# RWKV shift and gated-DeltaNet convolution read from PSUM, state copies by ScalarE, five kinds of stores on GpSimd's queue

## The chip, the cores and the metric

The kernel runs on one core of a Trainium2 chip. The metric is the time on the device of one execution, in microseconds (us). A core has five engines, each of which works through its own list of instructions in order: TensorE (PE, the matrix engine, whose results land in banks of PSUM), VectorE (DVE), ScalarE (ACT), GpSimd (POOL) and SyncE (SP, which here only issues transfers). They meet through semaphores: an instruction that waits holds up everything behind it on its engine.

## The reference

One step of a hybrid decoder of two layers, width 1024, on 512 prompt tokens and 32 sample tokens (8 sequences of 4) that share the weights. In each layer one projection `h @ w_in` is split into four mixers. Two parts of it matter here. RWKV mixes each token's projection with that of the token before it, and the gated DeltaNet runs a convolution of width 4 along time:

```python
prev = jnp.concatenate([shift_buf, p[:, :-1]], axis=1)      # rwkv7_mixer
xs = p + (prev - p) * prm['rw_mu']
...
xp = jnp.concatenate([buf, x], axis=1)                      # causal_dwconv
y = sum(xp[:, i:i + L] * w[i] for i in range(width))
return y, xp[:, L:]
```

The last row of `p` and the last three rows of `x` are outputs too (the new shift and convolution states). The sample tokens take their earlier rows from `state_rwkv_shift` and `state_gdn_conv`; the prompt starts from zeros.

## The kernel before

Everything is kept transposed: features on the 128 partitions, tokens along the free dimension. The tokens are worked on in two halves: half 0 is the prompt's first 256 columns, half 1 the other 256 and the 32 sample columns (288). So there are four projections, written (layer, half): (0,0), (0,1), (1,0), (1,1). In the execution shown, RWKV's and the DeltaNet's units are evacuated at about 24 to 78 us for (0,0), 141 to 213 us for (0,1), 640 to 697 us for (1,0) and 1037 to 1085 us for (1,1).

A projection is a row of units of 128 output features. A unit's weights come as two half units of 128x512 numbers (`load_part`): SP's queue loads one into `wraw` (five buffers), ScalarE rounds it into `whi`, VectorE subtracts to get `wlo` (three buffers each). TensorE makes 24 matmuls per unit in `dense`: high weights on the high and the low part of the input, low weights on the high part. They add up in one PSUM bank of the tag `mm`, of which there are three, so a unit's bank must be free again before the third unit after it can start. `evac` then takes the unit out of the bank.

`rw_evac` (units 0 to 7) and `gd_evac` (units 10 to 15) first copy the bank by ScalarE into a tile `raw` (shown as `e`) with room ahead of the columns for the row or rows before. GpSimd fills that room (zeros, or `rwlast` and `rwshift`, `gdlast` and `gdconv`) and copies the new states out at the end (`rwlast`, `rwshs`, `gdlast`, `gdcs`). ScalarE writes the scaled projection to `xs` or `cv`, and VectorE adds the shifted rows with one `scalar_tensor_tensor` per tap (`stt`, listed at line 245, the helper's), over `raw` whole.

A small ninth piece, `narrow`, loads 8 gate columns (`wnar`) through SP's queue, L1689. Also on SP's queue are the stores of two S5 tables (`m1` at L1337, `s5en` at L1396, both made by GpSimd in `tables`) and of the residual `x` at L1653.

The order on each engine is laid out by a scheduler when the program is built, from priorities that the sections carry (the evacuation's is 1050, the load's 294); the engines keep to it when they run.

Of the kernel before, what the change touches and what calls it, by code (L numbers as in the profile page):

```python
# [11 lines left out]
AF = mybir.ActivationFunctionType  # L12
ALU = mybir.AluOpType
# [3 lines left out]
DEPTH, D, SEQ, DB, DS = 2, 1024, 512, 8, 4  # L17
NS = DB * DS
# [121 lines left out]
class K:  # L140
# [16 lines left out]
    def t(self, shape, tag, bufs=1, dt=F32, pool="sb"):  # L157
# [1 line left out]
        return self.pool(pool).tile(list(shape), dt, tag=tag, name=f"{tag}_{self.n}", bufs=bufs)  # L159


    CLS = {"c0": (640, 7), "c1": (1152, 4), "e1": (1280, 2), "d1": (1152, 2), "d2": (2304, 2), "sums": (1152, 3),
           "xs": (9216, 1), "r2": (2304, 5), "r4": (4096, 5),
           "cv": (6912, 1), "gz": (2304, 1), "g2": (2304, 5), "g4": (4608, 1),
           "t2": (2048, 5), "s0": (4096, 1),
# [205 lines left out]
    def rw_evac(self, r, u, ps):  # L371

        nc = self.nc
        half, xs = r["half"], r["xs"]
        mu = self.p("rw_mu")[:, u:u + 1]
        om = self.rwd[:, u:u + 1]
        raw = self.w([128, 1 + 256 + DB + NS], "e1")
        self.acopy(raw[:, 1:257], ps[:, :256])
        if not half:
            nc.gpsimd.memset(raw[:, 0:1], 0.0)  # L380
        else:
            nc.gpsimd.tensor_copy(raw[:, 0:1], self.rwlast[:, u:u + 1])
            nc.gpsimd.tensor_copy(raw[:, 257:257 + DB], self.rwshift[:, u])
            self.acopy(raw[:, 257 + DB:], ps[:, 256:])
            self.act(xs[:, u, 256:], ps[:, 256:], AF.Copy, scale=om)
            self.stt(xs[:, u, 256:], raw[:, 257:257 + NS], mu, xs[:, u, 256:], ALU.mult, ALU.add)
            nc.gpsimd.tensor_copy(self.rwshs[:, u], raw[:, 257 + NS:])
        if u in (4, 5):

            sw = lambda a: a.rearrange("p (b c t) -> p b c t", b=2, c=2)  # L390
            xo, pi, pp = sw(xs[:, u, 0:256]), sw(raw[:, 0:256]), sw(ps[:, :256])
            for c in range(2):
                self.act(xo[:, :, 1 - c], pp[:, :, c], AF.Copy, scale=om)
                self.stt(xo[:, :, 1 - c], pi[:, :, c], mu, xo[:, :, 1 - c], ALU.mult, ALU.add)
# [372 lines left out]
    def gd_evac(self, r, u, ps):  # L767
        nc = self.nc
        half, cv = r["half"], r["cv"]
        w = lambda i: self.p("gdn_conv_w")[:, i * 6 + u:i * 6 + u + 1]  # L770
        raw = self.w([128, 3 + 256 + 3 * DB + NS], "e1")
        if not half:
            nc.gpsimd.memset(raw[:, 0:3], 0.0)  # L773
        else:
            nc.gpsimd.tensor_copy(raw[:, 0:3], self.gdlast[:, u])
            nc.gpsimd.tensor_copy(raw[:, 259:259 + 3 * DB], self.gdconv[:, u])
            self.acopy(raw[:, 259 + 3 * DB:], ps[:, 256:])
        self.acopy(raw[:, 3:259], ps[:, :256])
# [481 lines left out]
    def s5_tables(self, l):  # L1260
        nc = self.nc
        V = self.t([128, 16, 8], "s5v", bufs=1)
        k = lambda j: V[:, j]
# [13 lines left out]
        c1 = 6.28125  # L1277
# [42 lines left out]
        kx, m1 = (self.w([128, 2, 8, 16, 4], "r4") for _ in range(2))  # L1320
# [53 lines left out]
        en = self.w([128, 2, 8, 64], "r4")  # L1374
        nc.gpsimd.memset(en[:, 0, :, 0:1], 1.0)
        nc.gpsimd.memset(en[:, 1, :, 0:1], 0.0)
        w, cur, nxt = 1, (V[:, 14], V[:, 15]), (V[:, 12], V[:, 13])
        while w < 64:
# [3 lines left out]
            a = (en[:, 0, :, 0:w], en[:, 1, :, 0:w])  # L1382
            o = (en[:, 0, :, w:2 * w], en[:, 1, :, w:2 * w])
# [243 lines left out]
    def residual(self, half, src, sums, cls, final=False, wide=True):  # L1627


        c0, n = HALVES[half]  # L1630
        xt = self.fetch(half, cls)
        rs = self.rms(sums)
        step = 2 if final else 4
        new = None if final else self.row(half, "sums")
        mp = None
        for q in range(0, 8, step):
            a, xq = src[:, q:q + step], xt[q // 4][:, q % 4:q % 4 + step]
            self.tt(a, a, rs.unsqueeze(1).to_broadcast([128, step, n]))
# [401 lines left out]
```

## Time and profile before

| | |
|---|---|
| median of 3 runs | 1650.72 us (1645.68 to 1654.04) |
| profiled execution | 1647.81 us, span of the trace 1646.0 us |
| TensorE busy | 1560.8 us, 95% of the span |
| VectorE, ScalarE, GpSimd busy | 74%, 59%, 19% |
| mean granted TensorE clock | 0.978 |

The page's chain that ended last is of little use for this change, since it shows only the end. What tells is, stage by stage, how much of a window TensorE was idle, and what it waited for there.

### The profile page before, as it was taken

The numbers are of one execution on the slowest core, as the hardware profiler recorded it, in microseconds if no ns is written. First come the engines' busy times: TensorE is split into PE (matmuls) and PEld (weight loads), VectorE is DVE, ScalarE is ACT, GpSimd is POOL, SyncE is SP. The second block draws the span as 40 slices with busy tenths as digits, with TensorE's granted clock in tenths as the row PEclk, the third lists the DMA queues.
The fourth block names the chain that finished last, engine by engine and source line by source line (L and its number), as shares of the span: only waits on it lengthen the run. The fifth ranks groups of instructions, "written<-read, shape, count | busy, mean of one in ns | idle before, by whom it ended". The sixth has DMA issues, their size and how long they took to land. (4 is left out here: it accounts for less than half of the span.)

```text
span 1646.0 us, 38658 instructions
## 1 busy us (share of the span) xinstructions
PE 1560.8 (95%) x14464; PEld 1454.1 (88%) x14464; DVE 1210.5 (74%) x2865; ACT 964.8 (59%) x2094; POOL 311.5 (19%) x614
## 2 busy tenths in 40 slices
PE   6989999899999999799999999999999999999996
PEld 6878987788898999788889999989889989999996
DVE  6799775876786868778586667889768865866665
ACT  6676556653355468575455567876444456855544
POOL 4661232000230424600020002520002101100001
PEclk9999998899999999899999999999999999999998
DMA  6635443443466566435356546534534755665453
GB/s 216 198 108 130 150 152 122 119 107 111 140 217 213 194 206 232 129 94 148 117 179 194 164 161 208 176 125 139 151 113 148 250 194 194 205 193 167 160 170 103
DMA packets 205415, 267.36 MB, mean 162 GB/s; under 512 B 81114, under 2 KB 98844, under 8 KB 204812
## 3 DMA queue, kind: packets, MB, share of 16 engines
q1 hardware_dynamic: 203308, 258.73, 49.8%
q0 software_dynamic: 1920, 6.17, 1.0%
q8 instruction: 113, 1.85, 0.5%
q14 instruction: 74, 0.61, 0.1%
HBM read 237.95 MB, written 28.58 MB: 162 GB/s over the span
## 5 line engine op out<-in xcount | busy, mean ns | idle before, releaser
L232 ACT CAST whi<-wraw 128x512 fp32r<-128x512 f32 x752 | 463.0, 619 | 426.0 <-PE ps L220 267.4
L236 DVE TENSOR_TENSOR wlo<-wraw,whi 128x512 fp32r<-128x512 f32 x752 | 535.6, 718 | 211.6 <-ACT whi L232 189.3
L220 PE MATMUL ps<-h,whi 128*128 128x288 f32 (+1 forms) x3264 | 515.3, 297 | 9.3 <-ACT h L228 4.3
L220 PEld LDWEIGHTS ps<-h,whi 128*128 128x128 f32 x3264 | 451.7, 192 | 24.8 <-ACT h L228 5.7
L220 PE MATMUL ps<-f,whi 128*128 128x288 f32 (+1 forms) x2752 | 425.4, 294 | 6.9 <-ACT whi L232 2.8
L220 PEld LDWEIGHTS ps<-f,whi 128*128 128x128 f32 x2752 | 374.3, 190 | 19.8 <-issue 5.4
L220 PE MATMUL ps<-h,wlo 128*128 128x288 f32 (+1 forms) x1632 | 289.7, 296 | 3.0 <-DVE wlo L236 2.7
L220 PEld LDWEIGHTS ps<-h,wlo 128*128 128x128 f32 x1632 | 236.6, 191 | 12.8 <-DVE wlo L236 5.6
L220 PE MATMUL ps<-f,wlo 128*128 128x288 f32 (+1 forms) x1376 | 237.6, 294 | 6.4 <-DVE wlo L236 6.3
L220 PEld LDWEIGHTS ps<-f,wlo 128*128 128x128 f32 x1376 | 197.3, 190 | 11.6 <-DVE wlo L236 7.6
L236 POOL TENSOR_TENSOR sums<-sums,d 128x288 f32<-128x288 f32 (+1 forms) x60 | 60.9, 1016 | 530.7 <-ACT d L228 525.1
L236 DVE TENSOR_TENSOR acc<-acc,ps 128x256 f32<-128x256 f32 (+1 forms) x96 | 41.6, 434 | 52.9 <-PE ps L220 52.5
L220 PE MATMUL ps<-r,r 64*64 64x64 f32 (+7 forms) x1184 | 68.4, 237 | 10.3 <-DMA r<-s5m 3.3
L220 PEld LDWEIGHTS ps<-r,r 64*64 64x64 f32 (+4 forms) x1184 | 56.5, 141 | 20.3 <-issue 9.0
L232 ACT CAST f<-d 128x288 fp32r<-128x288 f32 (+1 forms) x128 | 53.4, 417 | 30.8 <-DVE d L236 30.4
L228 ACT ACTIVATE d<-ps 128x256 f32<-128x256 f32 (+1 forms) x156 | 61.3, 393 | 14.0 <-PE ps L220 12.8
L228 ACT ACT_TABLE_LOAD x45 | 57.7, 1283 | 0.8
L236 DVE TENSOR_TENSOR f<-d,f 128x288 fp32r<-128x288 f32 (+1 forms) x128 | 55.5, 433 | 2.9 <-ACT f L232 2.5
L236 DVE TENSOR_TENSOR d<-d 128x288 f32<-128x288 f32 (+1 forms) x128 | 55.7, 435 | 1.5 <-ACT d L228 1.5
L232 ACT COPY e<-ps 128x256 f32<-128x256 f32 (+2 forms) x96 | 27.9, 324 | 17.9 <-PE ps L220 8.4
L245 DVE SCALAR_TENSOR_TENSOR cv<-e,pf,cv 128x256 f32<-128x256 f32 (+1 forms) x90 | 32.4, 403 | 7.4 <-POOL e L773 4.3
L232 ACT COPY r<-ps 64x128 f32<-64x128 f32 (+2 forms) x56 | 20.4, 370 | 29.2 <-PE ps L625 12.1
(395 smaller groups left out, 1852.8 us busy)
## 6 DMA issues: line engine op xcount, KB each, us to landing
wraw<-in_w_up SPq DMA_DIRECT2D x256, 256.0 KB, 2.8
wraw<-in_w_down SPq DMA_DIRECT2D x256, 256.0 KB, 2.8
wraw<-in_w_in SPq DMA_DIRECT2D x176, 256.0 KB, 3.1
wraw<-in_w_out SPq DMA_DIRECT2D x64, 256.0 KB, 3.0
t<-diag SPq DMA_DIRECT2D x32, 128.0 KB, 3.2
x<-acc SPq DMA_DIRECT2D x3, 1152.0 KB, 5.6
x<-acc SPq DMA_DIRECT2D x3, 1024.0 KB, 5.1
xs<-mix SPq DMA_DIRECT2D x8, 288.0 KB, 3.0
```

Source lines behind the costliest of these rows:

```text
L220: return self.nc.tensor.matmul(out=out, lhsT=lhsT, rhs=rhs, start=start, stop=stop)
L228: return self.nc.scalar.activation(out=out, in_=in_, func=func, scale=scale, bias=bias, **kw)
L232: return self.nc.scalar.copy(out, in_)
L236: return (eng or self.nc.vector).tensor_tensor(out=out, in0=a, in1=b, op=op)
L245: return self.nc.vector.scalar_tensor_tensor(out=out, in0=a, scalar=s, in1=b, op0=op0, op1=op1)
```

## The change

`rw_evac` and `gd_evac` no longer make `raw`. VectorE's taps read the PSUM bank, and the columns whose earlier row lies elsewhere become short instructions of their own. RWKV in half 1: 255 columns from the bank, 1 from `rwlast`, 24 from the bank, 8 from `rwshift` (units 4 and 5, which lie reversed, take five pieces where there were two, and two more for the first column and the samples). The convolution in half 1: for each of three taps four instructions instead of two, k, 256 - k, 8k and 32 - 8k columns wide. In half 0 the count stays, apart from units 4 and 5. GpSimd's copies and fills go; the new states are copied by ScalarE from the bank. The stores of `m1`, `s5en` and `x` are issued by GpSimd instead of SP. Line numbers after the change are two lower from `gd_evac_z` on.

```diff
 rw_evac:
-        raw = self.w([128, 1 + 256 + DB + NS], "e1")
-        self.acopy(raw[:, 1:257], ps[:, :256])
-        if not half:
-            nc.gpsimd.memset(raw[:, 0:1], 0.0)
-        else:
-            nc.gpsimd.tensor_copy(raw[:, 0:1], self.rwlast[:, u:u + 1])
-            nc.gpsimd.tensor_copy(raw[:, 257:257 + DB], self.rwshift[:, u])
-            self.acopy(raw[:, 257 + DB:], ps[:, 256:])
...
-            xo = xs[:, u, 0:256]
-            self.act(xo, ps[:, :256], AF.Copy, scale=om)
-            self.stt(xo, raw[:, 0:256], mu, xo, ALU.mult, ALU.add)
-        nc.gpsimd.tensor_copy(self.rwlast[:, u:u + 1], raw[:, 256:257])
+        shift = lambda o, a: self.stt(o, a, mu, o, ALU.mult, ALU.add)
...
+            self.act(xs[:, u], ps, AF.Copy, scale=om)
+            shift(xs[:, u, 1:256], ps[:, 0:255])
+            x0 = xs[:, u, 0:1]
+        if half:
+            shift(x0, self.rwlast[:, u:u + 1])
+            shift(xs[:, u, 256 + DB:], ps[:, 256:256 + NS - DB])
+            shift(xs[:, u, 256:256 + DB], self.rwshift[:, u])
+            self.acopy(self.rwshs[:, u], ps[:, 256 + NS - DB:])
+        self.acopy(self.rwlast[:, u:u + 1], ps[:, 255:256])
 gd_evac:
-        raw = self.w([128, 3 + 256 + 3 * DB + NS], "e1")
...
         self.act(cv[:, u], ps, AF.Copy, scale=w(3))
         for i in range(3):
-            self.stt(cv[:, u, 0:256], raw[:, i:i + 256], w(i), cv[:, u, 0:256], ALU.mult, ALU.add)
+            tap = lambda o, a: self.stt(o, a, w(i), o, ALU.mult, ALU.add)
+            k = 3 - i
+            tap(cv[:, u, k:256], ps[:, 0:256 - k])
             if half:
-                o = 259 + i * DB
-                self.stt(cv[:, u, 256:], raw[:, o:o + NS], w(i), cv[:, u, 256:], ALU.mult, ALU.add)
-        nc.gpsimd.tensor_copy(self.gdlast[:, u], raw[:, 256:259])
+                tap(cv[:, u, 0:k], self.gdlast[:, u, i:])
+                tap(cv[:, u, 256 + k * DB:], ps[:, 256:256 + NS - k * DB])
+                tap(cv[:, u, 256:256 + k * DB], self.gdconv[:, u, i * DB:])
+        self.acopy(self.gdlast[:, u], ps[:, 253:256])
         if half:
-            nc.gpsimd.tensor_copy(self.gdcs[:, u], raw[:, 259 + NS:])
+            self.acopy(self.gdcs[:, u], ps[:, 256 + NS - 3 * DB:])
 tables, twice, and the store of x (here en's):
-        self.nc.sync.dma_start(out=ten, in_=en.rearrange("p x a c -> p (x a c)"))
+        self.nc.gpsimd.dma_start(out=ten, in_=en.rearrange("p x a c -> p (x a c)"))
```

VectorE's list in projection (1,1), among the DeltaNet's units. `cv` gathers the convolution, `e_2809` and `e_2817` are `raw` of the second and first units then open. Before, from the half unit `wlo_14940` to the next, `wlo_14958`:

```order
L236 TENSOR_TENSOR wlo_14940<-wraw_14938,whi_14939 128x512
L245 SCALAR_TENSOR_TENSOR cv_14731<-e_2809_14770,pf_75,cv_14731 128x256
L245 SCALAR_TENSOR_TENSOR cv_14731<-e_2817_14821,pf_75,cv_14731 128x256
L245 SCALAR_TENSOR_TENSOR cv_14731<-e_2817_14821,pf_75,cv_14731 128x32
L236 TENSOR_TENSOR wlo_14958<-wraw_14956,whi_14957 128x512
L245 SCALAR_TENSOR_TENSOR cv_14731<-e_2809_14770,pf_75,cv_14731 128x32
L236 TENSOR_TENSOR wnar_2852_15041<-wnar_15040,wnar_2852_15041 128x8x8
```

After, the same half unit is `wlo_14822`. `ps_14611`, `ps_14663` and `ps_14715` are the banks of the first, second and third DeltaNet unit:

```order
L236 TENSOR_TENSOR wlo_14822<-wraw_14820,whi_14821 128x512
L245 SCALAR_TENSOR_TENSOR cv_14609<-ps_14715,pf_75,cv_14609 128x253
L245 SCALAR_TENSOR_TENSOR cv_14609<-gdlast_9384,pf_75,cv_14609 128x3
L245 SCALAR_TENSOR_TENSOR cv_14609<-ps_14715,pf_75,cv_14609 128x8
L245 SCALAR_TENSOR_TENSOR cv_14609<-gdconv_9382,pf_75,cv_14609 128x24
L245 SCALAR_TENSOR_TENSOR cv_14609<-ps_14663,pf_75,cv_14609 128x254
L245 SCALAR_TENSOR_TENSOR cv_14609<-gdlast_9384,pf_75,cv_14609 128x2
L245 SCALAR_TENSOR_TENSOR cv_14609<-ps_14663,pf_75,cv_14609 128x16
L245 SCALAR_TENSOR_TENSOR cv_14609<-gdconv_9382,pf_75,cv_14609 128x16
L245 SCALAR_TENSOR_TENSOR cv_14609<-ps_14611,pf_75,cv_14609 128x255
L245 SCALAR_TENSOR_TENSOR cv_14609<-gdlast_9384,pf_75,cv_14609 128x1
L245 SCALAR_TENSOR_TENSOR cv_14609<-ps_14611,pf_75,cv_14609 128x24
```

Before, three taps stood between the two half units; now there are 24 and the narrow piece's subtraction, and the last tap that reads the first unit's bank, `ps_14611`, is among the first twelve of them (its two last pieces follow the rows shown).

ScalarE's list at the same place, before, from the second unit's scaling to the third's copies:

```order
L228 ACTIVATE cv_14731<-ps_14784,pf_75 128x288
L232 CAST whi_14939<-wraw_14938 128x512
L232 CAST whi_14957<-wraw_14956 128x512
L232 CAST wnar_2852_15041<-wnar_15040 128x8x8
L232 CAST whi_14990<-wraw_14989 128x512
L232 CAST whi_15008<-wraw_15007 128x512
L232 COPY e_2825_14872<-ps_14835 128x32
L232 COPY e_2825_14872<-ps_14835 128x256
```

And after, from the third unit's scaling on; `whi_14839` is the half unit that was `whi_14957`:

```order
L228 ACTIVATE cv_14609<-ps_14715,pf_75 128x288
L232 CAST wnar_2796_14925<-wnar_14924 128x8x8
L232 COPY gdlast_9384<-ps_14611 128x3
L232 COPY gdcs_9385<-ps_14611 128x24
L232 COPY gdlast_9384<-ps_14663 128x3
L232 COPY gdcs_9385<-ps_14663 128x24
L232 COPY gdlast_9384<-ps_14715 128x3
L232 COPY gdcs_9385<-ps_14715 128x24
L232 CAST whi_14839<-wraw_14838 128x512
```

The copies of the new states of three units now stand, behind the narrow piece, ahead of that half unit's rounding, and the first two of them are the last to read the first unit's bank.

SP's list at the end of the DeltaNet's units in projection (1,0), before:

```order
L1662 DMA wraw_9692<-in_w_in 128x512
L1662 DMA wraw_9710<-in_w_in 128x512
L1396 DMA s5en_1732_9090<-r_1714_9009 128x1024
L1689 DMA wnar_9737<-in_w_ba 128x64
L1662 DMA wraw_9761<-in_w_in 128x512
L1662 DMA wraw_9779<-in_w_in 128x512
```

After:

```order
L1660 DMA wraw_9599<-in_w_in 128x512
L1660 DMA wraw_9617<-in_w_in 128x512
L1687 DMA wnar_9641<-in_w_ba 128x64
L1660 DMA wraw_9665<-in_w_in 128x512
L1660 DMA wraw_9683<-in_w_in 128x512
L1660 DMA wraw_9705<-in_w_in 128x512
```

The store of `s5en` no longer stands ahead of `wnar`. It is now on GpSimd's list, behind the instructions that make what it stores:

```order
L236 TENSOR_TENSOR d_1702_9024<-r_1686_8951,s5v_8768 128x256
L236 TENSOR_TENSOR d_1703_9028<-r_1686_8951,s5v_8768 128x256
L236 TENSOR_TENSOR r_1686_8951<-r_1686_8951,d_1702_9024 128x8x32
L236 TENSOR_TENSOR r_1686_8951<-r_1686_8951,d_1703_9028 128x8x32
L1394 DMA s5en_1704_9032<-r_1686_8951 128x1024
L412 MEMSET c_1892_9998 1x256
```

Its wait for `r_1686` is thus one of GpSimd for itself.

## Rows read from the trace of the kernel before

**Rows 1.** The page: busy time, share of span, and instructions of each engine.
```profile
PE 1560.8 (95%) x14464; PEld 1454.1 (88%) x14464; DVE 1210.5 (74%) x2865; ACT 964.8 (59%) x2094; POOL 311.5 (19%) x614
```

**Rows 2.** Windows: busy us of each engine (instructions), clock, DMA share, GB/s.
```profile
24.00:54.00 30.00, 25.78 (x201) 24.28 (x200) 24.27 (x44) 18.59 (x44) 26.08 (x65) 0.97 0.58 188
...
142.00:182.00 40.00, 40.00 (x476) 35.36 (x475) 29.53 (x90) 24.22 (x72) 10.28 (x34) 1.00 0.56 162
182.00:222.00 40.00, 40.00 (x529) 36.09 (x529) 30.67 (x89) 20.36 (x46) 6.96 (x24) 1.00 0.38 120
660.00:693.00 33.00, 24.41 (x171) 22.97 (x171) 24.99 (x44) 18.53 (x41) 24.15 (x57) 0.84 0.44 141
1062.00:1085.00 23.00, 23.00 (x174) 22.08 (x172) 22.24 (x61) 16.34 (x41) 12.71 (x29) 1.00 0.52 166
```

**Rows 3.** Waits, 660 to 693: waiter, awaited, total us, times, longest.
```profile
PE ps L220 <- DVE wlo L236: 5.6, 3, 3.0
PE ps L220 <- ACT cv L228: 2.7, 1, 2.7
...
ACT wnar L232 <- DMA wnar<-in_w_ba: 8.2, 1, 8.2
...
DVE cv L245 <- POOL e L773: 4.3, 2, 2.2
...
SPq L1396 <- POOL r L236: 8.8, 1, 8.8
```

**Rows 4.** Timeline, 660 to 693: start, us, instructions [idle before, releaser].
```profile
681.28 1.23 PE L220 MATMUL ps<-f,wlo 128*128 128x256 f32 x4 [3.02 <-DVE wlo L236]
...
682.70 0.33 SPq L1396 DMA_DIRECT2D s5en<-r  x1
...
686.34 0.24 ACT L232 CAST wnar<-wnar 128x64 fp32r<-128x64 f32 x1 [8.17 <-DMA wnar<-in_w_ba]
...
687.80 2.08 PE L220 MATMUL ps<-f,whi 128*128 128x256 f32 x8 [2.74 <-ACT cv L228]
...
690.53 1.17 PE L220 MATMUL ps<-f,whi 128*128 128x256 f32 x8
```

**Rows 5.** Timeline, same columns, 40 to 60: ScalarE, then TensorE.
```profile
47.40 0.38 ACT L232 COPY e<-ps 128x256 f32<-128x256 f32 x1 [4.32 <-POOL rwlast L399]
...
51.86 0.77 PE L220 MATMUL ps<-rww,c 65*128 65x256 f32 x2 [1.23 <-ACT c L228]
```

**Rows 6.** VectorE groups: count, busy us, mean ns, idle before.
```profile
L245 DVE SCALAR_TENSOR_TENSOR cv<-e,pf,cv 128x256 f32<-128x256 f32 x54 | 26.9, 509 | 7.3 <-POOL e L773 4.3 <-ACT cv L228 1.2 <-POOL gdlast L785 0.6
...
L245 DVE SCALAR_TENSOR_TENSOR cv<-e,pf,cv 128x32 f32<-128x32 f32 x36 | 8.6, 244 | 0.0
...
L245 DVE SCALAR_TENSOR_TENSOR rwS<-ps,rwee,rwSE 128x64 f32<-128x64 f32 x28 | 6.6, 277 | 4.0 <-PE ps L220 4.0
```

**Rows 7.** ScalarE and GpSimd groups, same columns.
```profile
L232 ACT COPY e<-ps 128x256 f32<-128x256 f32 x62 | 23.2, 374 | 12.8 <-POOL rwlast L399 6.6 <-PE ps L220 5.7 <-issue 0.2
...
L232 ACT COPY e<-ps 128x32 f32<-128x32 f32 x28 | 5.5, 196 | 3.1 <-PE ps L220 2.7 <-DVE cv L245 0.5
...
L399 POOL COPY rwlast<-e 128x1 f32<-128x1 f32 x32 | 19.1, 598 | 60.6 <-ACT e L232 60.5
...
L1821 POOL DMA_DIRECT2D diag<-r x4 | 2.4, 608 | 0.0
```

**Rows 8.** Timeline, 1062 to 1083: TensorE and VectorE.
```profile
1068.34 0.69 PE L220 MATMUL ps<-f,wlo 128*128 128x288 f32 x4
...
1068.87 1.22 PE L220 MATMUL ps<-f,whi 128*128 128x288 f32 x8
...
1070.05 0.68 DVE L236 TENSOR_TENSOR wlo<-wraw,whi 128x512 fp32r<-128x512 f32 x1
...
1080.14 2.89 DVE L245 SCALAR_TENSOR_TENSOR cv<-e,pf,cv 128x256 f32<-128x256 f32 x9
...
1082.95 0.68 DVE L236 TENSOR_TENSOR wlo<-wraw,whi 128x512 fp32r<-128x512 f32 x1
```

More of the change, by code (lines that the diff above doesn't have):

```diff
@@ L159, in t @@
         return self.pool(pool).tile(list(shape), dt, tag=tag, name=f"{tag}_{self.n}", bufs=bufs)
-    CLS = {"c0": (640, 7), "c1": (1152, 4), "e1": (1280, 2), "d1": (1152, 2), "d2": (2304, 2), "sums": (1152, 3),
+    CLS = {"c0": (640, 7), "c1": (1152, 4), "e1": (1152, 2), "d1": (1152, 2), "d2": (2304, 2), "sums": (1152, 3),
            "xs": (9216, 1), "r2": (2304, 5), "r4": (4096, 5),
@@ L376, in rw_evac @@
         om = self.rwd[:, u:u + 1]
-        raw = self.w([128, 1 + 256 + DB + NS], "e1")
-        self.acopy(raw[:, 1:257], ps[:, :256])
-        if not half:
-            nc.gpsimd.memset(raw[:, 0:1], 0.0)
-        else:
-            nc.gpsimd.tensor_copy(raw[:, 0:1], self.rwlast[:, u:u + 1])
-            nc.gpsimd.tensor_copy(raw[:, 257:257 + DB], self.rwshift[:, u])
-            self.acopy(raw[:, 257 + DB:], ps[:, 256:])
-            self.act(xs[:, u, 256:], ps[:, 256:], AF.Copy, scale=om)
-            self.stt(xs[:, u, 256:], raw[:, 257:257 + NS], mu, xs[:, u, 256:], ALU.mult, ALU.add)
-            nc.gpsimd.tensor_copy(self.rwshs[:, u], raw[:, 257 + NS:])
+        shift = lambda o, a: self.stt(o, a, mu, o, ALU.mult, ALU.add)
         if u in (4, 5):
             sw = lambda a: a.rearrange("p (b c t) -> p b c t", b=2, c=2)
-            xo, pi, pp = sw(xs[:, u, 0:256]), sw(raw[:, 0:256]), sw(ps[:, :256])
+            xo, pp = sw(xs[:, u, 0:256]), sw(ps[:, :256])
             for c in range(2):
                 self.act(xo[:, :, 1 - c], pp[:, :, c], AF.Copy, scale=om)
-                self.stt(xo[:, :, 1 - c], pi[:, :, c], mu, xo[:, :, 1 - c], ALU.mult, ALU.add)
-        else:
-            xo = xs[:, u, 0:256]
-            self.act(xo, ps[:, :256], AF.Copy, scale=om)
-            self.stt(xo, raw[:, 0:256], mu, xo, ALU.mult, ALU.add)
-        nc.gpsimd.tensor_copy(self.rwlast[:, u:u + 1], raw[:, 256:257])
+            if half:
+                self.act(xs[:, u, 256:], ps[:, 256:], AF.Copy, scale=om)
+            for c in range(2):
+                shift(xo[:, :, 1 - c, 1:], pp[:, :, c, 0:63])
+            shift(xo[:, :, 0, 0], pp[:, :, 0, 63])
+            shift(xo[:, 1, 1, 0:1], pp[:, 0, 1, 63:64])
+            x0 = xo[:, 0, 1, 0:1]
+        else:
+            self.act(xs[:, u], ps, AF.Copy, scale=om)
+            shift(xs[:, u, 1:256], ps[:, 0:255])
+            x0 = xs[:, u, 0:1]
+        if half:
+            shift(x0, self.rwlast[:, u:u + 1])
[3 more added lines that the diff above has]
+        self.acopy(self.rwlast[:, u:u + 1], ps[:, 255:256])
     def rw_stage1(self, l, r):
@@ L770, in gd_evac @@
         w = lambda i: self.p("gdn_conv_w")[:, i * 6 + u:i * 6 + u + 1]
-        raw = self.w([128, 3 + 256 + 3 * DB + NS], "e1")
[L772 to L778, printed above, removed]
         self.act(cv[:, u], ps, AF.Copy, scale=w(3))
         for i in range(3):
-            self.stt(cv[:, u, 0:256], raw[:, i:i + 256], w(i), cv[:, u, 0:256], ALU.mult, ALU.add)
+            tap = lambda o, a: self.stt(o, a, w(i), o, ALU.mult, ALU.add)
+            k = 3 - i
+            tap(cv[:, u, k:256], ps[:, 0:256 - k])
             if half:
-                o = 259 + i * DB
-                self.stt(cv[:, u, 256:], raw[:, o:o + NS], w(i), cv[:, u, 256:], ALU.mult, ALU.add)
-        nc.gpsimd.tensor_copy(self.gdlast[:, u], raw[:, 256:259])
+                tap(cv[:, u, 0:k], self.gdlast[:, u, i:])
+                tap(cv[:, u, 256 + k * DB:], ps[:, 256:256 + NS - k * DB])
+                tap(cv[:, u, 256:256 + k * DB], self.gdconv[:, u, i * DB:])
+        self.acopy(self.gdlast[:, u], ps[:, 253:256])
         if half:
-            nc.gpsimd.tensor_copy(self.gdcs[:, u], raw[:, 259 + NS:])
+            self.acopy(self.gdcs[:, u], ps[:, 256 + NS - 3 * DB:])
     def gd_evac_z(self, r, u, ps):
@@ L1336, in s5_tables @@
         tab = [self.t([128, n], f"s5{nm}{l}", pool="dram", bufs=1) for nm, n in (("kin", 1024), ("m1", 1024), ("m2", 512))]
-        self.nc.sync.dma_start(out=tab[1], in_=m1.rearrange("p x a b c -> p (x a b c)"))
+        self.nc.gpsimd.dma_start(out=tab[1], in_=m1.rearrange("p x a b c -> p (x a b c)"))
         gp = self.ps([128, 8, 4, 16])
@@ L1652, in residual @@
         self.x[half] = self.t([128, 8, n], f"x{half}", pool="dram", bufs=2)
-        self.nc.sync.dma_start(out=self.x[half], in_=src)
+        self.nc.gpsimd.dma_start(out=self.x[half], in_=src)
         return self.rsqrt(new, mp, m) if wide else self.rms(new)
```

## The prediction

> **What bounds the kernel now.** First the page's busy times: TensorE is busy 1560.8 us of 1646.0 [rows 1], so only the other 85 us can be won, and any delay that TensorE cannot fill is lost. Then windows over the four evacuations [rows 2]. In (0,0), 24 to 54 us, TensorE is busy 25.78 of 30 us while GpSimd is busy 26.08. In (0,1) it is busy all 80 us of two windows, with VectorE at 29.53 and 30.67 of 40 each. In (1,0), 660 to 693 us, it is busy 24.41 of 33 at a mean granted clock of 0.84, with GpSimd at 24.15. In (1,1), 1062 to 1085 us, it is busy 23.00 of 23 and VectorE 22.24. The change touches two stages with gaps and two without. Then the waits in the worst window [rows 3], and the timeline there, to see which of them ends last [rows 4].
>
> **(1,0), half 0, layer 1.** TensorE's idle time is 33 - 24.41 = 8.6 us, and nearly all is named: 5.6 us for `wlo` and 2.7 us for a scaled `cv` [rows 3]. Two chains lie behind it, and the change cuts both. VectorE's taps wait 4.3 us for GpSimd to fill the head of `e` and hold the next `wlo` behind them [rows 3]; GpSimd is then working on the S5 tables. And SP waits 8.8 us for GpSimd's `r` to store `s5en` [rows 3]; `wnar`, next in its list, lands late, ScalarE stands 8.17 us before `wnar`'s rounding, and TensorE 2.74 us for what is queued behind it [rows 4]. The first idle stretch of that size is at 681.28 (3.02 us). The clock is low here too: eight matmuls of one form take 2.08 us at 687.80 and 1.17 at 690.53 [rows 4], levels of 1.2 and 2.4 GHz, so each such group at the low level costs 0.9 us; about three groups' worth, 2.5 us, is what this window lost to it. All that could come back is 8.6 + 2.5 = 11 us.
>
> Not all of it will. The taps now hold the PSUM bank: the fourth DeltaNet unit reuses the first one's, which is free only when VectorE has made all three of its taps and ScalarE has copied `gdlast`. Scaling the third unit, a `wlo` (0.68 us [rows 8]), up to nine taps at 0.41 to 0.51 us, and the copy come to some 4 us after the third unit's matmuls; and `wnar`, which lands 3.3 us after its issue (about 683.1 to 686.34), still stands ahead of the copies on ScalarE. Ends: -10 (both chains gone, nothing new) and -1 (the bank takes the place of both). I take -5, since the new wait is of the size of half the old.
>
> **(0,0), half 0, layer 0.** TensorE is idle 4.2 us in 30 [rows 2]. ScalarE waits 4.32 us at 47.40 for GpSimd's `rwlast`, and TensorE's largest gap, 1.23 us at 51.86, follows four microseconds later on ScalarE's `c` [rows 5]. With the copy of `e` gone that wait goes. Ends -4 and +1 (a held bank); I take -2.
>
> **(1,1), half 1, layer 1.** Here the order decides. The first DeltaNet unit's bank must be free for the fourth unit. Before, `raw` freed it early: TensorE went on at 1068.87 without a gap, straight behind 1068.34 [rows 8]. Now its last tap stands twelve instructions behind a `wlo` which itself needs the buffer that the third unit's last matmuls free, and two ScalarE copies follow. The prices: `wlo` 0.68 [rows 8]. A tap of 256 columns has a mean of 0.48 to 0.51 us and one of 32 columns 0.244 [rows 6]; but nine of them in a row, mixed, took from 1080.14 to the next instruction's start at 1082.95 [rows 8], 2.81 us, where five long and four short ones by their means would be 3.4. So in a row each costs some 0.07 less: 0.41 and 0.17. Three long and nine short ones (most are under 32 columns wide) are 3 x 0.41 + 9 x 0.17 = 2.8 us, at most 3 x 0.51 + 9 x 0.244 = 3.7. The copies: 128x32 took 196 ns [rows 7], two are 0.4. Sum: 0.7 + 2.8 + 0.4 = 3.9, about 4 us with the hand-overs, in which TensorE has nothing else in its list. A gap of that kind can lower the clock, as in (1,0): 0 to 3 us more; I take half. (1,1): +5.5, ends +2 and +10.
>
> Reading PSUM by VectorE costs no more than reading SBUF: `rwS` from a bank, 64 columns wide, takes 277 ns, and the line through 244 (32 columns) and 479 (the low end at 256) gives 278 for 64 [rows 6].
> The Trainium skill, Perfetto Trace Analysis, Optimizing Scalar/DVE Operations, puts VectorE's overhead per instruction at about 60 ns on SBUF and 125 ns on PSUM, which speaks against this change; the row at 64 columns does not agree. By that page the six taps among those twelve that read a bank would add 6 x 65 ns = 0.4 us to (1,1), an estimate.
>
> **(0,1), half 1, layer 0.** VectorE gets 36 more taps in the DeltaNet and 20 more pieces in RWKV. At 0.13 us net each (two short ones stand for one of 244 ns now and then) this is some 7 us on an engine at 60 of 80 us, beside a TensorE without a gap [rows 2]. TensorE has mixer matmuls of half 0 to fill in here, which (1,1) at that place has not, so only part of a 4-us hold reaches it. +3, ends 0 and +8.
>
> **The rest.** ScalarE loses 56 copies of 374 ns and 28 of 196 ns [rows 7], 26 us, and gains 84 tiny ones of under 196 ns, at most 16 us. Its gain lies beside a busy TensorE: nothing. GpSimd loses 60 us of small work, `rwlast` alone 19.1 us [rows 7], all beside the path outside (0,0) and (1,0). Ten stores cost GpSimd about 0.6 us each [rows 7] where it is mostly idle; SP is freed of their waits ahead of weight loads, which rarely come last, as weights are five buffers ahead. 0, ends -3 and +3; the latter also for a scheduler that has laid out every stage anew.
>
> **Sum.** -5 - 2 + 5.5 + 3 + 0 = +1.5 us on the profiled 1647.8 us: 1649.3. The median of the runs shown is 2.9 us above the profiled one, so the forecast is 1652 us: no change that can be told. A measurement of this kernel tells about 0.5%, 8 us, from no change (its own runs spread by 8.4 us).
>
> **Rivals.**
> A, slower: held banks. In both half-1 stages each DeltaNet unit from the fourth on, and RWKV's too, finds its bank held, and the low clock follows every gap. For it: VectorE at 22.24 of 23 us [rows 2], which gets 3 to 4 us of taps there, more than fits. Against it: in (0,1) TensorE has other work. Price: (1,1) +10, (0,1) +8, and the gain in (1,0) only 2 and in (0,0) none: +16, 1667 us by the median. It decides from the point where VectorE is over its window, so that `wlo` itself comes late after the gap.
>
> B, faster: GpSimd out of the chain is the whole story. (1,0) gives 10, (0,0) 4, the stores 2, and (1,1)'s gap is 4 without a fall of the clock, (0,1) 0: -12, 1639 us. For it: GpSimd at 24.15 of 33 and 26.08 of 30 us in just the two stages with gaps [rows 2], and all four waits of [rows 3]. Against it: the fourth unit's bank in (1,0).
>
> C, the change doesn't do what it says: taking GpSimd off leaves the wait for `wnar` as long as before, since it is the transfer that comes last, and (1,0) gains only the 2 to 3 us of the taps' wait. The other terms as taken: about +4, 1654 us, inside the forecast's own band.
>
> **How the numbers follow.** The forecast, with C beside it, has 0.48; A 0.27; B 0.25. The forecast's own ends, added as independent (4.5, 2.5, 4, 4 and 3 us), give about 8 us either way: 1644 to 1660. The range that leaves out 2 in 10 goes from B's middle to a little under A's: 1637 to 1665. Faster by over 0.5% is below 1642.5: most of B and a few parts of the forecast, 0.26. Slower is above 1659: most of A and a few parts of the forecast, 0.28. The rest is 0.46.
>
> **What would show it.** In (1,1) a gap of TensorE of about 4 us ahead of the fourth DeltaNet unit's first matmuls, released by ScalarE's `gdcs` or `gdlast`, and a granted clock below 1.00 behind it: without the gap this term is wrong. In (1,0) no wait of VectorE for GpSimd, `wnar` rounded with a wait well under 8 us, idle time of 3 to 5 us instead of 8.6, and the largest part of it ended by a copy of `gdlast`. In (0,1) TensorE's two full windows lose a few us. VectorE's taps from PSUM cost by width what the line says. What would make the forecast wrong: gaps after every DeltaNet unit in half 1 (A), or a full (1,0) at a clock of 1.00 (B).

## The result

The changed kernel takes 1664.15 us (median of 4 runs, 1662.15 to 1667.81), before 1649.35 us: a ratio of 1.0096, with a 95% interval of 1.0074 to 1.0118. It is slower by 0.96%, where no change that can be told was forecast. The profiled execution took 1667.81 us (span 1666.0), 20.0 us more than the one of before. Single profiles of one kernel differ by some us. Ratios are estimated from all the runs, so they need not be the quotient of the two medians; places are from the profiles.

The page of the changed kernel, which answers to [rows 1]:

```profile
PE 1568.8 (94%) x14464; PEld 1461.2 (88%) x14464; DVE 1220.2 (73%) x2985; ACT 957.6 (57%) x2085; POOL 269.5 (16%) x456
```

VectorE has 9.7 us more, ScalarE 7 less, GpSimd 42 less. None of this says where 20 us went. To see that, both traces are cut where VectorE starts the same half units of the weights (`wlo`, counted from 0). The windows of before, from half unit 44 to 88 (projection (0,1)), to 200 and to 232 (layer 0's other mixers and MLP), then 248 to 292 ((1,0)), 440 to 470 (the end of RWKV and the DeltaNet in (1,1)), and 470 to 500; the columns as in [rows 2]:

```profile
120.26:257.65 137.39, 130.52 (x1518) 117.36 (x1515) 109.30 (x316) 78.84 (x196) 39.95 (x120) 0.96 0.48 142
257.65:551.55 293.90, 276.55 (x2820) 244.76 (x2820) 221.99 (x586) 157.57 (x349) 45.16 (x61) 0.97 0.47 149
551.55:601.42 49.87, 49.39 (x441) 48.09 (x441) 38.15 (x65) 32.00 (x70) 12.42 (x11) 1.00 0.60 186
...
632.70:734.57 101.87, 87.45 (x670) 80.98 (x669) 79.31 (x167) 70.47 (x151) 43.73 (x97) 0.93 0.43 143
...
1034.65:1089.88 55.23, 55.23 (x405) 53.62 (x404) 46.57 (x115) 44.17 (x113) 27.14 (x57) 1.00 0.54 175
1089.88:1160.22 70.34, 69.27 (x588) 62.83 (x586) 60.91 (x179) 52.41 (x121) 4.66 (x9) 1.00 0.46 132
```

The same of the changed kernel:

```profile
119.99:261.93 141.94, 132.31 (x1494) 118.90 (x1491) 114.42 (x359) 73.34 (x181) 24.22 (x57) 0.95 0.46 136
261.93:558.02 296.09, 277.20 (x2761) 245.67 (x2761) 214.59 (x586) 156.53 (x346) 35.76 (x54) 0.95 0.47 146
558.02:614.98 56.96, 52.72 (x494) 51.34 (x495) 44.58 (x66) 32.82 (x71) 25.04 (x19) 1.00 0.55 170
...
646.05:739.98 93.93, 84.72 (x692) 79.35 (x691) 80.42 (x182) 69.56 (x153) 38.14 (x70) 0.98 0.48 158
...
1039.91:1105.38 65.47, 59.77 (x421) 57.22 (x420) 53.88 (x176) 45.42 (x113) 3.35 (x6) 0.97 0.44 144
1105.38:1176.28 70.90, 68.89 (x573) 62.08 (x573) 60.36 (x178) 49.72 (x117) 4.77 (x9) 0.98 0.46 132
```

The second number is the window's length. (0,1) costs 4.6 us more, the stretch to 200 2.2, that to 232 7.1; (1,0) gains 7.9; the two windows of (1,1) lose 10.2 and 0.6. The first 44 half units and those from 232 to 248 and 292 to 440 are level within 0.3 us; after 500 another 3.8 is lost. Matmuls that moved over a border shift some us between neighbours: the stretch to 200 has 59 fewer than before and that to 232 has 53 more, so these two are best read together, 9.3 us.

**The held bank, as forecast.** The changed kernel's timeline in (1,1): TensorE's last matmuls of the third DeltaNet unit, a `wlo` and a tap that VectorE still has in hand, the `wlo` behind them, the last piece of a tap that reads the first unit's bank, ScalarE's two copies, TensorE's fourth unit.

```profile
1073.95 0.69 PE L220 MATMUL ps<-f,wlo 128*128 128x288 f32 x4
...
1074.67 0.70 DVE L236 TENSOR_TENSOR wlo<-wraw,whi 128x512 fp32r<-128x512 f32 x1
...
1075.27 0.49 DVE L245 SCALAR_TENSOR_TENSOR cv<-ps,pf,cv 128x254 f32<-128x254 f32 x1
...
1076.08 0.70 DVE L236 TENSOR_TENSOR wlo<-wraw,whi 128x512 fp32r<-128x512 f32 x1
...
1078.81 0.26 DVE L245 SCALAR_TENSOR_TENSOR cv<-ps,pf,cv 128x24 f32<-128x24 f32 x1
...
1079.10 0.16 ACT L232 COPY gdlast<-ps 128x3 f32<-128x3 f32 x1 [1.94 <-DVE cv L245]
1079.16 0.18 ACT L232 COPY gdcs<-ps 128x24 f32<-128x24 f32 x1
...
1079.40 2.29 PE L220 MATMUL ps<-f,whi 128*128 128x288 f32 x8 [4.76 <-ACT gdcs L232]
```

The gap is 4.76 us and ends with `gdcs`. Of it 1.44 us pass before the `wlo` at 1076.08, which stands in VectorE's list behind an earlier `wlo` and four pieces of a tap; that `wlo` and the pieces up to the copies take 3.02, the copies 0.30. The unit's first matmuls then take 2.29 us, where the same eight took 1.22 before [rows 8]: the low level of the clock. In (1,0) there is one gap of the same kind, with `wnar`'s wait now 1.89 us:

```profile
685.23 0.24 ACT L232 CAST wnar<-wnar 128x64 fp32r<-128x64 f32 x1 [1.89 <-DMA wnar<-in_w_ba]
...
686.68 0.16 ACT L232 COPY gdlast<-ps 128x3 f32<-128x3 f32 x1 [1.21 <-DVE cv L245]
...
686.89 2.07 PE L220 MATMUL ps<-f,whi 128*128 128x256 f32 x8 [4.88 <-ACT gdlast L232]
```

It replaces the waits of [rows 3], 8.3 us, and so (1,0) still gains: in the window of 101.87 us TensorE's idle time falls from 14.4 to 9.2 us, and the mean clock rises from 0.93 to 0.98.

**Losses that were not forecast.** Near 80 us, in (0,0), VectorE's pair `r` holds back `wlo`, and TensorE stands 5.30 us. From the timeline of the changed kernel:

```profile
77.46 5.50 DVE L245 SCALAR_TENSOR_TENSOR r<-acc,pf,r 128x256 f32<-128x256 f32 x2 [1.20 <-ACT r L228]
...
80.36 1.18 POOL L236 TENSOR_TENSOR r<-r,s5v 128x256 f32<-128x256 f32 x2
81.51 1.18 POOL L236 TENSOR_TENSOR d<-r,s5v 128x256 f32<-128x256 f32 x2
...
85.95 1.22 PE L220 MATMUL ps<-h,wlo 128*128 128x256 f32 x4 [5.30 <-DVE wlo L236]
```

Before, the same pair took 3.07 us, beside narrower ones:

```profile
85.02 3.07 DVE L245 SCALAR_TENSOR_TENSOR r<-acc,pf,r 128x256 f32<-128x256 f32 x2 [0.32 <-ACT r L228]
```

And from 564 to 580 us VectorE's instructions take 1.5 to 1.6 us in the mean while GpSimd makes layer 1's S5 tables (`s` and `r`, 128x512). VectorE's groups there (count, busy us, mean ns):

```profile
L236 DVE TENSOR_TENSOR wlo<-wraw,whi 128x512 fp32r<-128x512 f32 x6 | 9.4, 1566 | 0.3 <-ACT whi L232 0.3
L236 DVE TENSOR_TENSOR d<-d 128x256 f32<-128x256 f32 x3 | 4.6, 1540 | 0.0
L236 DVE TENSOR_TENSOR f<-d,f 128x256 fp32r<-128x256 f32 x2 | 3.2, 1622 | 0.0
```

Before, the same table work lay at 539 to 560 us, mostly beside a down part of the MLP. VectorE's `wlo` were as slow there (536 to 560 us):

```profile
L236 DVE TENSOR_TENSOR wlo<-wraw,whi 128x512 fp32r<-128x512 f32 x13 | 19.6, 1545 | 0.2 <-ACT whi L232 0.2
```

But the down part asks for little else of VectorE, 13 of them came out in 24 us, and TensorE was idle for 0.5 us from 539 to 560 and for 0.5 from half unit 200 to 232 (49.87 - 49.39). Now the work lies beside an up part, `d` and `f` stand between the `wlo`, only 6 come out in 16 us, and TensorE idles 4.2 us.

Between half units 88 and 200, too, there are two gaps that before has not, each with the low clock behind it (TensorE's timeline, then windows from the ends of the gaps on):

```profile
340.28 0.33 PE L220 MATMUL ps<-t,t 64*64 64x64 f32 x2 [2.26 <-DMA t<-diag]
...
470.94 0.47 PE L220 MATMUL ps<-r,r 64*64 64x72 f32 x8 [2.27 <-POOL r L236]
```

```profile
340.00:350.00 10.00, 9.72 (x92) 9.04 (x94) 4.77 (x17) 1.90 (x4) 0.00 (x0) 0.66 0.08 27
...
470.80:476.00 5.20, 5.06 (x46) 4.85 (x48) 2.49 (x6) 1.11 (x2) 3.23 (x4) 0.67 0.48 162
```

Counting half of TensorE's busy time in spells at the low level, the clock costs 13.3 us in that stretch, for 7.8 before, and idle time grows by 1.5 us.

### The profile page after: what moved, and what is told of

The parts are those of the page before. It is cut to its first block, busy times and chain, and to the rows that moved or that the text cites. A ratio compares the mean times of both kernels' runs of the same rounds, so it can differ in the third digit from the quotient of the medians.

```text
span 1666.0 us, 38507 instructions
## 1 busy us (share of the span) xinstructions
PE 1568.8 (94%) x14464; PEld 1461.2 (88%) x14464; DVE 1220.2 (73%) x2985; ACT 957.6 (57%) x2085; POOL 269.5 (16%) x456
## 5 line engine op out<-in xcount | busy, mean ns | idle before, releaser
L220 PEld LDWEIGHTS ps<-h,wlo 128*128 128x128 f32 x1632 | 238.2, 193 | 20.8 <-DVE wlo L236 14.4
L236 DVE TENSOR_TENSOR d<-d 128x288 f32<-128x288 f32 (+1 forms) x128 | 59.9, 468 | 0.0
L220 PE MATMUL ps<-t,t 64*64 64x64 f32 x1024 | 36.6, 221 | 3.8 <-DMA t<-diag 3.7
L220 PEld LDWEIGHTS ps<-t,t 64*64 64x64 f32 x1024 | 32.7, 135 | 8.1 <-DMA t<-diag 4.3
```

The lines of the kernel that those rows point to most:

```text
L220: return self.nc.tensor.matmul(out=out, lhsT=lhsT, rhs=rhs, start=start, stop=stop)
L236: return (eng or self.nc.vector).tensor_tensor(out=out, in0=a, in1=b, op=op)
```

## The experiments

Theory 1: the taps hold banks, which costs a gap in each second-layer projection, and the rest of the loss is the scheduler's new layout of other stages. The rivals: the stores on GpSimd's queue cost; VectorE's extra instructions cost; the reading of PSUM costs. Ratios are to before, on the same chip, with 95% intervals; medians of different batches come from different chips.

**The parts.** `s_only`: only the three stores move (`m1`, `s5en` and `x` are all that the change moves; the title's five is a miscount).

```diff
-        self.nc.sync.dma_start(out=ten, in_=en...)
+        self.nc.gpsimd.dma_start(out=ten, in_=en...)
```

> Only the stores of m1, s5en and x go to GpSimd's queue; the evacuations are as before. Theory 1 (banks held by the taps lose 4 to 5 us each at two places, and the rest of the loss is a new layout of the stages around): faster by 3 to 8 us, since SP's 8.8-us wait in (1,0) goes and 12 of its 33 us had a wait or a low clock; no gap of 4 us ahead of the fourth DeltaNet unit in (1,1). Theory 2 (the stores on GpSimd's queue cost, since GpSimd's own work stands behind them): slower by 5 us or more, with the S5 tables of layer 1 later against the weights. If neither: within 3 us.

Measured 1648.67 us, 0.9987 (0.9966 to 1.0008). The stores alone do nothing that can be told; theory 2 is out, and theory 1's 3 us gain is not shown either. In its profile (1,0), half units 248 to 292, does take 99.6 us for 101.9.

`rw_only`: only `rw_evac` as in the change.

> Only rw_evac reads PSUM; the DeltaNet's evacuation and the stores are as before. Theory 1: no gap ahead of the fourth DeltaNet unit in (1,1) and (1,0); -3 to +3 us from the evacuations themselves, and what the new layout of the other stages gives, up to 10 us either way. Theory 2: no change beyond 3 us, because the stores stay on SP.

Measured 1657.18 us, 1.0048 (1.0024 to 1.0071). In (1,1), from half unit 440 to 470, TensorE idles 0.5 us, as expected. It idles 5.0 us between 200 and 232, although no RWKV evacuation lies there. Against the expectation there is a gap of 7.81 us in (1,0), ended by ScalarE's `cv` behind a wait of 9.63 us for `wnar`, whose load stands behind the store of `s5en`, still on SP's queue.

`gd_only`: only `gd_evac` as in the change.

> Only gd_evac reads PSUM; RWKV's evacuation and the stores are as before. Theory 1: gaps of TensorE of 4 to 5 us ahead of the fourth DeltaNet unit in (1,0) and (1,1), released by ScalarE's copies of the states; (1,1) loses 5 to 9 us, (1,0) little, in all +5 to +12 us. Theory 2: no change beyond 3 us.

Measured 1678.57 us, 1.0173 (1.0146 to 1.0200), worse than the whole change and, at some 28 us, more than twice the 5 to 12 us expected. The gap in (1,1) is there (4.65 us). That in (1,0) is 14.44 us, three times what was expected.

`rw_gd`: both evacuations, stores on SP.

> Both evacuations read PSUM, the stores stay on SP. Theory 1: slower by about what the whole change is (15 us) and some 5 us more, because in (1,0) wnar stays behind the store of s5en. Theory 2: within 5 us of before.

Measured 1677.03 us, 1.0171 (1.0141 to 1.0200), some 28 us where about 20 was expected. From its timeline in (1,0):

```profile
688.86 0.33 SPq L1394 DMA_DIRECT2D s5en<-r  x1
689.72 0.79 SPq L1687 DMA_DIRECT2D wnar<-in_w_ba  x1
...
692.80 0.24 ACT L232 CAST wnar<-wnar 128x64 fp32r<-128x64 f32 x1 [10.02 <-DMA wnar<-in_w_ba]
692.96 0.15 ACT L232 COPY gdlast<-ps 128x3 f32<-128x3 f32 x1
...
693.16 2.08 PE L220 MATMUL ps<-f,whi 128*128 128x256 f32 x8 [12.95 <-ACT gdlast L232]
```

So the parts don't add. The stores, worth nothing alone, are worth 8 us of gap (12.95 against 4.88) once the copy that frees a bank stands behind `wnar` on ScalarE: the wait for `s5en` then reaches TensorE undiminished.

**Bank or VectorE's count?** `sbuf_split`: the change, but the DeltaNet's taps, in the same pieces, read a copy.

```diff
+        raw = self.w([128, 256 + NS * half], "e1")
+        self.acopy(raw, ps)
         self.act(cv[:, u], ps, AF.Copy, scale=w(3))
-            tap(cv[:, u, k:256], ps[:, 0:256 - k])
+            tap(cv[:, u, k:256], raw[:, 0:256 - k])
```

> The change, but the DeltaNet's taps, in the same pieces, read a copy of the bank in SBUF that ScalarE makes first; the states are copied from it too. Theory 1 (what loses time in the last DeltaNet stage is the bank held until the last tap): the gap of 4.76 us ahead of the fourth DeltaNet unit in (1,1) goes or is under 1.5 us, and so is the 4.88-us one in (1,0); 5 to 10 us faster than the change. Rival (VectorE's 36 more taps per layer are what costs): the gap stays above 3 us, since VectorE's list is as long as with the change.

Measured 1654.60 us, 1.0002 (0.9973 to 1.0031). Its window from half unit 440 to 470:

```profile
1033.96:1090.16 56.20, 55.18 (x402) 53.26 (x401) 51.50 (x165) 42.44 (x111) 2.82 (x5) 1.00 0.54 167
```

56.20 us against 65.47 of the change and 55.23 of before, with VectorE's 165 instructions near the change's 176, and busy 51.50 us of it. From half unit 440 to 500 idle time and low clock cost 1.0 us, for 10.8 in the change and 1.1 before. The bank was the cost, not the count: VectorE has room for the pieces when nobody waits for a bank. A gap of 4.65 to 4.76 us is there in all five kernels whose taps in half 1 read the bank in pieces, and in the other thirteen TensorE idles 1.1 us or less in that window. In (1,0) less came back than expected: a gap of 2.20 us is left ahead of the fourth unit, ended by `cv`, where under 1.5 was expected. The total, by the ratios some 15 us below the change, is more than the 5 to 10 expected, but the intervals leave room for 10.

**Layout alone.** `before_gdt`: before, with one priority changed.

```diff
-PRIO = {... 'gdt': 200}
+PRIO = {... 'gdt': 400}
```

> The kernel before with one number of the scheduler's table changed (gdt 200 to 400); no evacuation, no store and no instruction is touched. In its TensorE list the last matmuls of the DeltaNet's sample step of layer 0, behind which GpSimd's S5 tables of layer 1 start, stand at half unit 199 of the weights, as in the changed kernel, not at 191 as before. Theory 1 (outside the evacuations the loss is the new layout: GpSimd's S5 tables now run beside an up part of the MLP, where VectorE has more to do): TensorE idle 4 to 5 us between half units 200 and 232, as with the change, where before has 0.5; the total 3 to 10 us above before. Rival (the loss there comes from the PSUM reads or the copies by ScalarE): idle below 1.5 us there, total within 3 us.

Measured 1654.66 us, 1.0046 (1.0011 to 1.0082). TensorE's waits in this kernel from 555 to 575 us, and the changed kernel's from 560 to 582 (us in total, times, longest):

```profile
PE ps L220 <- DVE wlo L236: 4.8, 5, 1.7
```

```profile
PE ps L220 <- DVE wlo L236: 4.2, 5, 1.7
```

The same wait, with no evacuation touched: this part of the loss, 4 us, is the place of the table work in the layout. `after_tdve`: the change, with the tables' products on VectorE.

```diff
-        e = nc.vector if not l else nc.gpsimd
+        e = nc.vector
```

> The change, with the sixteen products and sums of layer 1's S5 tables (128x512) made by VectorE instead of GpSimd, as they are in layer 0. Theory 1 (VectorE's instructions are slowed to 1.5 to 1.9 us beside GpSimd's, and this makes wlo late): VectorE's wlo there take 0.7 us again; the table work, 8 to 14 us of VectorE, is now in its own list, so that idle between 200 and 232 is 1 to 4 us instead of 4.2; total 0 to 4 us faster than the change. Rival (VectorE is simply full there): idle above 6 us.

Measured 1662.74 us, 1.0072 (1.0044 to 1.0099). TensorE's wait from 552 to 575 us, and VectorE's work there:

```profile
PE ps L220 <- DVE wlo L236: 0.3, 1, 0.3
```

```profile
559.14 2.14 DVE L236 TENSOR_TENSOR s<-r,s5rv 128x512 f32<-128x512 f32 x2
561.19 0.69 DVE L236 TENSOR_TENSOR wlo<-wraw,whi 128x512 fp32r<-128x512 f32 x1
```

VectorE does the table work as well and is not late: its instructions were slow because of GpSimd, not too many. In the total the 4 us don't show: the interval overlaps that of the change.

**Other ways, and combinations.** `raw_act` keeps before's copy and taps, with heads and states filled by ScalarE (`self.acopy(raw[:, 0:3], self.gdlast[:, u])` and the like) and the stores on GpSimd's queue.

> The kernel before, with its copy of the bank in SBUF and its taps, but the heads filled and the states copied by ScalarE (zeros by VectorE), GpSimd out of the evacuation, and the stores on GpSimd's queue. Theory 1: no held bank, no wait for GpSimd: no gap above 1.5 us in (1,1), idle in (1,0) 8 us or less, and the moved S5 tables still cost 4 us between half units 200 and 232 (its marker is at 199): -8 to +3 us against before. Rival (VectorE and ScalarE busier with small instructions is what costs): +5 us or more.

Measured 1655.37 us, 1.0035 (1.0005 to 1.0064): no gap in (1,1), 5.1 us idle between 200 and 232, but also a new gap of 9.93 us at 250 us, among the mixers, which I had not expected. The ratio is some 6 us, over the -8 to +3 expected, and with its interval (1 to 11 us) the rival, small instructions on VectorE and ScalarE, is not ruled out for this kernel. `raw_tdve` is the same with the tables on VectorE.

> Copies in SBUF, heads and states by ScalarE, stores on GpSimd's queue, layer 1's S5 tables on VectorE. The theory expects the 5.1 us between half units 200 and 232 to go to below 1 us and the total to come down by 3 to 6 us from the same kernel with the tables on GpSimd: 1646 to 1652 us.

Measured 1651.54 us, 1.0028 (1.0004 to 1.0051), the idle time between 200 and 232 at 0.1 us; against before hardly better than `raw_act`, so the 5 us don't show in the total.

`s_tdve`: stores and tables moved, evacuations of before.

> The kernel before, with the stores on GpSimd's queue and layer 1's S5 tables on VectorE. There GpSimd's table work lies beside a stretch that costs no idle time (0.4 us between half units 200 and 232), so the theory expects nothing from the tables: -5 to +1 us against before. Rival (GpSimd's table work costs wherever it lies): -6 us or more.

Measured 1647.48 us, 1.0008 (0.9994 to 1.0023): the tables cost nothing that can be told where they lay.

`sbuf_tdve`: `sbuf_split` with the tables on VectorE.

> The change with both counter-measures: the DeltaNet's taps read a copy of the bank in SBUF, and layer 1's S5 tables are made by VectorE. If the two losses are separate, their repairs add: 1664 - 9 (the copy) - 4 (the tables) = 1648 to 1653 us, level with before or a little faster; idle between 200 and 232 below 1 us, no gap over 1.5 us in (1,1). If they are one and the same, no faster than the copy alone.

Measured 1643.01 us, 0.9979 (0.9959 to 0.9999): the two repairs add up, from 1.0096 to a little below before, and a little under the 1648 to 1653 us expected. What the tables give on top of the copy isn't shown, since the interval overlaps that of `sbuf_split`.

**By halves.** `half0_tdve` takes the change's evacuation in half 0, before's in half 1, the stores on GpSimd and the tables on VectorE.

```diff
+    def gd_evac(self, r, u, ps):
+        return (self.gd_evac1 if r["half"] else self.gd_evac0)(r, u, ps)
```

> Half 0's evacuations as in the change (VectorE reads PSUM, the same number of taps), half 1's as before (a copy in SBUF, GpSimd fills the heads), the stores on GpSimd's queue, and the sixteen products and sums of layer 1's S5 tables on VectorE. Theory (the bank hurts only where the taps are split in four and TensorE is full; outside, the moved S5 tables): no gap in (1,1); idle and low clock in (1,0) 8 to 13 us against 19 of before; under 1.5 us idle between half units 200 and 232; -10 to 0 us against before. Rival (reading PSUM in half 0 costs too): at or above before, with a gap of 4 us or more in (1,0) ahead of the fourth DeltaNet unit.

Measured 1632.62 us, 0.9917 (0.9896 to 0.9938): faster than both kernels, by 0.8% and, by the two ratios, 1.8%. The expected fall in (1,0) came, from 19.3 to 12.0 us of idle time and low clock, though the 4.88-us gap is there too. `half0` is the same with the tables on GpSimd.

> Half 0's evacuations as in the change, half 1's as before, the stores on GpSimd's queue; the S5 tables of layer 1 stay on GpSimd (the marker behind which they start is at half unit 201). The theory expects the 4 to 5 us between half units 200 and 232 back, and so 1636 to 1640 us, 4 to 6 above the same kernel with the tables on VectorE. Rival (the gain of that kernel came from half 0's evacuations alone): within 2 us of it.

Measured 1641.25 us, 0.9933 (0.9904 to 0.9962). Idle from 200 to 232 is 5.7 us against 0.0, but the ratios' intervals overlap, so what the tables give here isn't shown by the times.

`half1_tdve` is the counterpart of `half0_tdve`.

> The counterpart: half 1's evacuations as in the change (taps split in pieces, from PSUM), half 0's as before, stores on GpSimd's queue, layer 1's S5 tables on VectorE. The theory expects the gap of 4 to 5 us ahead of the fourth DeltaNet unit in (1,1) with its low clock, and 2 to 6 us more in (0,1): 1653 to 1662 us. Rival (the loss of the change was in half 0, at 80 us and in (1,0)): 1648 us or less.

Measured 1676.18 us, 1.0145 (1.0114 to 1.0177). The gap in (1,1) is 4.74 us; the loss is larger than expected: from half unit 88 to 200 it lost 14.6 us more than before to idle time and low clock. The 2 to 6 us expected in (0,1) did not come: from half unit 44 to 88 it takes 136.6 us for 137.4 of before, with the same pieces of taps there as the change, which takes 141.9.

**The gaps at 80 us and in (1,0).** `half0_en`: `half0_tdve` with the last doublings of layer 0's S5 powers on VectorE.

```diff
-            e = nc.gpsimd
+            e = nc.vector if not l and w >= 16 else nc.gpsimd
```

> The kernel with half 0 read from PSUM and the tables on VectorE, and in layer 0 the last two doublings of the S5 powers (16 and 32 wide) also on VectorE. Theory (the gap of 5 us at 80 us is VectorE's two instructions held to 5.2 us beside GpSimd's): that pair takes 1 us, and the gap at 80 us is under 2 us; total 0 to 5 us faster, less what 12 more instructions cost VectorE. Rival (VectorE is full there): the gap stays above 4 us.

The pair in this kernel:

```profile
77.96 0.88 DVE L245 SCALAR_TENSOR_TENSOR r<-acc,pf,r 128x256 f32<-128x256 f32 x2 [0.58 <-ACT r L228]
...
81.82 0.75 PE L220 MATMUL ps<-h,wlo 128*128 128x256 f32 x4 [0.67 <-DVE wlo L236]
```

0.88 us for 5.22 in `half0_tdve`, and the gap 0.67 for 5.02: the cause of this gap is shown. Yet the whole took 1663.00 us, 1.0043 (1.0008 to 1.0079), slower than `half0_tdve` where up to 5 us faster was expected: by the same count the new layout lost 11.5 us more between half units 44 and 88, and some 25 more between 88 and 200.

The Trainium skill, SBUF — State Buffer, SBUF: two separate sides, says that a GpSimd instruction and a VectorE one with two inputs in SBUF share a pair of ports, which one holds to its end while the other waits. The trace agrees: 5.50 us beside GpSimd in the changed kernel and 0.88 here, without its wide instructions. It also shows VectorE waiting for more than one: its pair ended at 82.96 us, 0.3 us after the last of GpSimd's row (82.69).

`half0_gs`: `half0_tdve`, with the DeltaNet's taps of half 0 on a copy in SBUF.

> The kernel with half 0 read from PSUM and the tables on VectorE, but the DeltaNet's taps of half 0 read a copy in SBUF that ScalarE makes. Theory (bank held): the gap of 4.88 us ahead of the fourth DeltaNet unit in (1,0) falls below 2.5 us; total 1 to 5 us faster, if the new layout doesn't take it back elsewhere. Rival (wnar's landing is what ends that gap): it stays above 4 us.

Measured 1656.87 us, 1.0026 (1.0008 to 1.0045). The gap in (1,0) fell to 2.83 us, short of the 2.5 expected, and ended with ScalarE's `cv`. So the bank did end it, but was worth only 2 us of it. What is left goes through the copy, which has two buffers: ScalarE waits 3.52 us for VectorE's taps to free one.

```profile
698.43 0.37 ACT L232 COPY e<-ps 128x256 f32<-128x256 f32 x1 [3.52 <-DVE cv L245]
```

The new layout gave back more, some 17 us against `half0_tdve` between half units 88 and 200.

## Why the prediction was wrong

By its steps, against the windows (profiled executions):

- (1,1): +5.5 (+2 to +10) forecast, +10.8 measured. The mechanism, the place and the gap were right (4 us said, 4.76 found, ended by `gdcs`), the gap's size in part by luck: the sum began at `wlo`, without the 1.44 us of VectorE's earlier work ahead of it, and what it did count took 3.3 us for 3.9. The whole was short by the low clock in both windows (3.1 us, half of TensorE's busy time in two spells, where half of 3 was taken) and by small gaps. `sbuf_split` confirms the cause.
- (1,0): -5 (-10 to -1) forecast, -7.9 measured; 4.88 us ended by `gdlast`, as said. The low clock had cost the forecast's window 3.3 us, not 2.5. The forecast gave the gain to POOL's absence and the stores without parting them; `rw_gd` (103.4 us for 101.9) shows that without the stores it would have been a small loss.
- (0,0): -2 forecast, -0.3 measured. ScalarE's wait for `rwlast` went, and a 5.30-us gap came that I had not seen. VectorE's pair took 3.07 us before too, beside other S5 instructions of GpSimd; in the new order it met the widest of them.
- (0,1): +3 (0 to +8) forecast, +4.6 measured, but by luck. The reason given, VectorE's pieces and held banks, isn't what the runs show: no gap of TensorE over 0.3 us there ends with a copy of a state (the two largest, 2.62 and 1.82 us, end with ScalarE's `e` and GpSimd's `r`, among the mixers), `half1_tdve` has the pieces and no loss, and `half0` has none of them and takes 141.2 us. What did cost it stays open.
- The price of PSUM: right. From a bank 253 columns took 477 ns and 24 took 241, from SBUF (`gdconv`) 24 took 239:

```profile
L245 DVE SCALAR_TENSOR_TENSOR cv<-ps,pf,cv 128x253 f32<-128x253 f32 x18 | 8.6, 477 | 0.2 <-ACT cv L228 0.2
...
L245 DVE SCALAR_TENSOR_TENSOR cv<-ps,pf,cv 128x24 f32<-128x24 f32 x12 | 2.9, 241 | 0.0
L245 DVE SCALAR_TENSOR_TENSOR cv<-gdconv,pf,cv 128x24 f32<-128x24 f32 x12 | 2.9, 239 | 0.0
```

- "The rest": 0 (-3 to +3) forecast, and about +12.8 measured (2.2 + 7.1 - 0.2 from half unit 88 to 248, -0.1 to 440, 3.8 after 500). This is the step that failed. It priced each part of the list at what it hides behind, and took GpSimd's work as lying beside the path wherever it was off the evacuations. But the change moves GpSimd's S5 tables, and beside a stage that needs VectorE they cost about 4 us (4.2 us idle for 0.5); `before_gdt` shows that cost without the change (4.8), `after_tdve` takes it out of the change (0.3). A new layout of all stages was in the forecast only as the upper end of +3. The order of the changed kernel was there to be read, and it had them eight half units later (199 for 191); I looked only at the evacuations.

Rival A had the time (1667 for 1664) but not the reason: in (1,1) one unit found its bank held, not each, (0,1) lost 4.6 and not 8, and more than half lay outside. Rival B's gain was real only in (1,0).

What stays open: of the 12.8 us, about 4 have a cause that is shown. Most of the rest is low clock between half units 88 and 200, 5.5 us more than before, in two spells behind the gaps at 340 and 471 us. `rw_gd` has both gaps with the stores on SP, so the stores are not their cause; what is isn't settled. Such gaps and spells differ from layout to layout by up to 25 us in one stretch (`half0_en` and `half0_tdve`). So it isn't shown either how much of `half0_tdve`'s 0.8% is its mechanism, and how much is a lucky layout: by the count of idle time and low clock it gains 11.5 us, 7.3 of them in (1,0) and 4.7 between half units 88 and 200, where no evacuation lies.

## What to carry to other kernels

Reading an accumulator in place saves a copy, but the copy was also what freed the bank: count what stands between the last matmul into a bank and its last reader, on every engine, before taking the copy out. Where two engines get in each other's way, work that an idle engine does for nothing in one stage costs in another; after a change that re-lays the program, look where such work has gone, not only at the lines that were edited. And a one-number change of the schedule is a cheap control for what a new layout alone does.

## What was not expected of the hardware

- VectorE's pair of 256 columns took 5.50 us beside GpSimd's wide tensor instructions and 0.88 us without; `wlo` took 1.57 us for 0.69.
- A change that does nothing alone (stores, 0.9987) was worth 0.75% in company (1.0171 to 1.0096), by 8 us of one gap and some of the layout.
